# Making the two one-hots of the gates on VectorE eight tokens at a time, with the gate multiplied in on ScalarE

## The chip, the cores and the metric

The kernel runs on one NeuronCore of one Trainium2 chip. The metric is the device time of one execution in microseconds. The core has five engines that matter here, each with an instruction queue of its own that is worked off in order: TensorE (PE, matrix products, with PEld for its weight loads), VectorE (DVE), ScalarE (ACT), GpSimd (POOL), and SyncE (SP), which only issues transfers. GpSimd issues transfers as well: the indirect fetches of this kernel.

## The reference

One layer of a hybrid encoder: attention and RWKV heads, an output projection, and then a PEER block, which is the part that matters here. For each of 1024 tokens, 8 heads each choose 16 of 16384 experts, so that a token has 128 experts with a number and a softmax weight each:

```
e_idx = i1 * 128 + i2                        # per token, 8 heads x 16
gate = jax.nn.softmax(top_s, axis=-1)
u = jnp.take(expert_u, ic, axis=0)
act = jax.nn.gelu(jnp.einsum('cd,ced->ce', xc, u), approximate=False)
vv = jnp.take(expert_v, ic, axis=0)
y = jnp.einsum('ce,ced->cd', gc * act, vv)
```

All inputs and outputs are float32.

## The kernel before, in words

The kernel computes the PEER block in two ways side by side. For the first three blocks of 128 tokens (`NGB = 3`) it fetches the rows of the chosen experts with indirect transfers, one expert of 128 tokens at a time. `fetch` (L1357) issues such a transfer on GpSimd, and VectorE then makes a dot product of 1024 columns per row of U (L1390) and adds a multiple of each row of V to `gacc` (L1398). For the other five blocks (640 tokens) it computes the activations of all 16384 experts as dense products (`act_half`, L1453) and multiplies them by a dense matrix of gates, which is zero where a token did not choose an expert.

That matrix of gates, `Gd` in DRAM, is made in a stage of its own, L1672 to L1762, called the gates stage below. `g_steps(b)` handles one block of 128 tokens. `prep` splits an expert's number into its upper and lower seven bits, transposes both and the gates on TensorE and copies them to the tile `tT`. Then 16 groups of eight tokens follow:

- `hot(t8)` makes, for each of the eight tokens, two one-hot matrices of 128 slots by 128 columns. `o2` has a one where the column is the lower half of the number. `o1` has the gate where the column is the upper half. `io128` holds 0 to 127 in each partition.
- `mm(t8)` multiplies `o1` by `o2` token by token on TensorE (L1733). The product is the token's 128 by 128 matrix of gates. ScalarE copies four tokens' results at a time from PSUM to the tile `st` (L1736), and after four groups SP stores `st` to `Gd` in eight pieces (L1745).

In the kernel before, `o2` is one VectorE instruction for eight tokens (L1706). `o1` is made token by token as the string `MIX = "DDDDPPAA"` tells: four tokens on VectorE and two on GpSimd with one compare-and-multiply each (L1712), and two on ScalarE with an absolute difference (L1718) and a rectified line (L1722), for which `prep` also writes the negated numbers and gates to `tT` (L1699, L1700). Both one-hots have `NHOT = 2` buffers, so `hot(k + 2)` can start only when `mm(k)` has read its tiles. The order of issue is `hot(k + 1)` ahead of `mm(k)`.

`merge` (L1761) lays three lists over the stage: the 80 groups, the dense products of the last 20 early tiles (`A(e2, NEARLY)`, 24 products of 128x128 by 320 columns three times over for each half tile, in L315 to L317), and 60 steps of fetched experts. Each such step has one fetch of U and one of V. A fetch is issued two steps ahead in the program (`LAG`). It also gets an ordering edge to the last instruction that was put into `pace[0]`: in the gates stage that is the last GpSimd one-hot (L1715), in the stage ahead of it the last `oe` product (L1628), in the stage behind it the last `gate` product (L1786). The edge orders instructions on GpSimd's queue and is no wait between engines.

After the gates stage the dense products with V begin (`one`, L1815), which load `Gd` back (`g_load`), multiply it in on GpSimd (`gate`) and run until the end of the kernel, with the rest of the fetches beside them.

Of the kernel before, what the change touches and what calls it, by code (L numbers as in the profile page):

```python
# [8 lines left out]
F32 = mybir.dt.float32  # L9
# [4 lines left out]
AF = mybir.ActivationFunctionType  # L14
ALU = mybir.AluOpType
# [5 lines left out]
D = 1024  # L21
# [46 lines left out]
TC = 32  # L68
NSTB = 2
STQ = 0  # L70
MIX = "DDDDPPAA"
HD = 64


# [5 lines left out]
def body(tc, nc, I, out, dbg=None):  # L80
# [3 lines left out]
    with root:  # L84
# [63 lines left out]
        def slot(name, shape=(128, 1024), dt=F32):  # L148
            return sp[1].tile(list(shape), dt, name=name, tag="s")
# [11 lines left out]
        def acp(o_, i_):  # L161
            nc.scalar.activation(o_, i_, AF.Copy)  # L162
# [56 lines left out]
        for k in range(NK):  # L219
            for i in range(2):  # L220
                a = slot("adw")
# [10 lines left out]
        for tb in range(NB):  # L232
# [5 lines left out]
            if tb % 4 == 3:  # L238
                r_ = rstd[:, tb - 3:tb + 1]
# [30 lines left out]
        def merge(*parts):  # L270

            o = []
            for n_, (steps, a_, b_) in enumerate(parts):
                for i, f in enumerate(steps):
                    o.append((a_ + (b_ - a_) * (i + 0.5) / len(steps), n_, i, f))
            for _, _, _, f in sorted(o, key=lambda z: z[:3]):
                f()
# [1011 lines left out]
        for tb in range(NB):  # L1289
# [7 lines left out]
            if tb % 2:  # L1297
                r_ = ss2[:, tb - 1:tb + 1]
                nc.vector.tensor_scalar(r_, r_, 1.0 / D, 1e-6, op0=ALU.mult, op1=ALU.add)
                rsqrt(r_, r_, [128, 2], "r1")  # L1300
                for b in range(tb - 1, tb + 1):
                    h_ = tl[f"h{b}"]
                    for hf in range(2):
                        cs_ = slice(hf * 512, hf * 512 + 512)
                        nc.vector.scalar_tensor_tensor(h_[:, cs_], h2[b][:, cs_], ss2[:, b:b + 1], sc2[hf],
                                                       op0=ALU.mult, op1=ALU.mult)
# [39 lines left out]
        io128 = pid.tile([128, 128], F32, name="io128")  # L1346
# [73 lines left out]
        pace = [None]  # L1420
# [54 lines left out]
        with ES() as qs:  # L1475
# [4 lines left out]
            def qbank(name):  # L1480
                return pq.tile([128, 512], F32, name=name, tag="b")
# [19 lines left out]
            pt = qbank("pt")  # L1501
# [164 lines left out]
            A = lambda a, b: sum(tl_[a:b], [])  # L1666
# [7 lines left out]
        with ES() as gs:  # L1674
            g1 = gs.enter_context(tc.tile_pool(name="g1", bufs=2, reuse_waits=TW))
            pg_ = gs.enter_context(tc.tile_pool(name="pgs", bufs=4, space=PSUM, reuse_waits=TW))

            stores = []
            if NXG:
                more.append((g1, NXG))  # L1680

            def g_steps(b):
                tb = NGB + b
                s = {}

                def prep():
                    ij = g1.tile([128, 2, 128], I32, name="ij", bufs=1)
                    nc.vector.tensor_scalar(ij[:, 0], eid[tb], 7, None, op0=ALU.logical_shift_right)
                    nc.vector.tensor_scalar(ij[:, 1], eid[tb], 127, None, op0=ALU.bitwise_and)
                    fj = g1.tile([128, 2, 128], F32, name="fj", bufs=1)  # L1690
                    nc.vector.tensor_copy(fj, ij)
                    pt = pg_.tile([128, 512], F32, name="ptg", tag="b")
                    nc.tensor.transpose(pt[:, 0:128], fj[:, 0], ident)
                    nc.tensor.transpose(pt[:, 128:256], fj[:, 1], ident)
                    nc.tensor.transpose(pt[:, 256:384], wgt[tb], ident)

                    s["t"] = tT = g1.tile([128, 5, 128], F32, name="tT")
                    acp(tT[:, 0:3].rearrange("p a b -> p (a b)"), pt[:, 0:384])
                    nc.scalar.activation(tT[:, 3], pt[:, 256:384], AF.Copy, scale=-1.0)  # L1699
                    nc.scalar.activation(tT[:, 4], pt[:, 0:128], AF.Copy, scale=-1.0)  # L1700

                def hot(t8):
                    tT = s["t"]
                    t0 = t8 * 8
                    s[t8] = o1, o2 = [g1.tile([128, 8, 128], F32, name=n_, bufs=NHOT) for n_ in ("o1", "o2")]
                    nc.vector.tensor_tensor(o2, io128[:, None, :].to_broadcast([128, 8, 128]),  # L1706
                                            tT[:, 1, t0:t0 + 8, None].to_broadcast([128, 8, 128]), ALU.is_equal)
                    for q in range(8):
                        t = t0 + q
                        if MIX[q] != "A":  # L1710
                            eng = nc.vector if MIX[q] == "D" else nc.gpsimd
                            r_ = eng.tensor_scalar(o1[:, q], io128, tT[:, 0, t:t + 1], tT[:, 2, t:t + 1],  # L1712
                                                   op0=ALU.is_equal, op1=ALU.mult)
                            if MIX[q] == "P":
                                pace[0] = r_  # L1715
                        else:

                            nc.scalar.activation(o1[:, q], io128, AF.Abs, bias=tT[:, 4, t:t + 1])  # L1718
                    for q in range(8):
                        t = t0 + q  # L1720
                        if MIX[q] == "A":
                            nc.scalar.activation(o1[:, q], o1[:, q], AF.Relu, scale=tT[:, 3, t:t + 1],  # L1722
                                                 bias=tT[:, 2, t:t + 1])

                def mm(t8):
                    if t8 % (TC // 8) == 0:
                        s["st"] = g1.tile([128, 128, TC], F32, name="st", bufs=NSTB)
                    st = s["st"]
                    o1, o2 = s[t8]
                    for x_ in range(2):  # L1730
                        pg = pg_.tile([128, 512], F32, name="pgb", tag="b")
                        for q in range(4):
                            nc.tensor.matmul(pg[:, q * 128:(q + 1) * 128], o1[:, 4 * x_ + q], o2[:, 4 * x_ + q],  # L1733
                                             start=True, stop=True)
                        t0 = t8 * 8 % TC + x_ * 4
                        nc.scalar.activation(st[:, :, t0:t0 + 4], pg.rearrange("p (q j) -> p j q", q=4), AF.Copy)  # L1736
                    for f in stores[:NPOP]:
                        f()
                    del stores[:NPOP]
                    if t8 * 8 % TC == TC - 8:  # L1740
                        stores.extend(lambda i=i: store(st, i, 128 // TC * b + t8 * 8 // TC) for i in range(NST))

                def store(st, i, c):
                    w = TC // NST
                    (nc.scalar if STQ else nc.sync).dma_start(  # L1745
                        Gd[w * i:w * i + w, :, c].rearrange("j i a t -> i j (a t)"),
                        st[:, TA * w * i:TA * w * i + TA * w].rearrange("p (j a) t -> p j (a t)", a=TA))

                L = [prep]
                for t8 in range(15 + NHOT):  # L1750
                    if t8 < 16:
                        L.append(lambda t8=t8: hot(t8))
                    if t8 >= NHOT - 1:
                        L.append(lambda t8=t8: mm(t8 - NHOT + 1))
                return L

            def flush():
                for f in stores:
                    f()

            merge((sum([g_steps(b) for b in range(ND)], []) + [flush], 0, WG[0]), (A(e2, NEARLY), WG[1], 1),  # L1761
                  (G_(NG3 - LAG) + [more.clear] + G_(LAG), 0, WG[2]))  # L1762
# [153 lines left out]
```

## Time and profile before

| what | value |
| --- | --- |
| time, median of 3 runs | 3918.12 us (3916.42 to 3923.77) |
| the profiled execution's own time | 3917.25 us |
| its span, first to last instruction | 3915.5 us |
| TensorE's mean granted clock | 0.925 of full speed |
| PE, PEld, DVE, ACT, POOL busy over the span | 85%, 75%, 77%, 32%, 49% |
| gates stage, first one-hot to last copy of gates | 1919.2 to 2349.6 us, 430.4 us |
| POOL, DVE, PE, ACT busy in it | 399.9, 353.9, 337.9, 239.2 us |

The shares of the whole span hide the stages. The gates stage is an eleventh of the span and the only part that the change touches; there the order of the engines is another than over the whole: GpSimd is the busiest. A busy time in the windows view counts time in which at least one instruction of the engine ran, so that instructions that overlap are counted once. In the groups by line, "mean ns" is the length of one instruction, overlap included.

### The profile page before, as it was taken

The page shows a single profiled execution, that of the slowest core. Times are in us where ns is not written, and L with a number is a line of the kernel's source. Part 1 is how long each engine was busy: PE and PEld are TensorE (multiplying, and loading weights), DVE is VectorE, ACT ScalarE, POOL GpSimd, SP SyncE. Part 2 cuts the span into 40 slices and gives each one's busy share as a digit, 9 for nine tenths or more (in the row PEclk, how much of TensorE's full clock was granted, in tenths as well). Part 3 has the DMA queues.
Part 4 walks back from the last instruction along what each step waited for, and adds up shares of the span by engine and source line. Part 5 has one row for each costly group of instructions (what it writes and reads, how often), then busy time and mean ns, then how long its engine had stood idle before and what let it go on. Part 6 is the DMA issues. An engine that isn't in the chain of part 4 may idle for free. (4 is left out here: it accounts for less than half of the span.)

```text
span 3915.5 us, 59807 instructions
## 1 busy us (share of the span) xinstructions
PE 3337.0 (85%) x21937; PEld 2929.5 (75%) x21937; DVE 3016.5 (77%) x6210; ACT 1248.9 (32%) x2400; POOL 1929.2 (49%) x1506
## 2 busy tenths in 40 slices
PE   5968899899697978878778777898999889998898
PEld 4747877777586978878777776777777777777777
DVE  6785557667647899999988886777777877788776
ACT  3234344445213322222355552222222222222221
POOL 2132111221334365456799996555555655555541
PEclk9988999899798988998999898999999999999999
DMA  6443434443455366566688889777777877777774
GB/s 198 178 135 123 141 95 121 101 105 94 110 185 190 97 213 219 170 218 227 209 287 282 280 288 328 285 282 290 294 292 293 300 284 290 295 297 298 291 269 158
DMA packets 493454, 862.68 MB, mean 220 GB/s; under 512 B 149348, under 2 KB 290404, under 8 KB 489064
## 3 DMA queue, kind: packets, MB, share of 16 engines
q1 hardware_dynamic: 372840, 447.20, 35.3%
q0 software_dynamic: 113280, 411.63, 28.9%
q8 instruction: 173, 2.83, 0.3%
q10 hardware_dynamic: 7040, 0.03, 0.1%
q14 instruction: 121, 0.99, 0.1%
HBM read 741.91 MB, written 116.80 MB: 219 GB/s over the span
## 5 line engine op out<-in xcount | busy, mean ns | idle before, releaser
L317 PE MATMUL pact<-dTh,uTl 128*128 128x320 f32 x2048 | 650.3, 319 | 51.6 <-DVE uTl L1450 51.4
L315 PE MATMUL pact<-dTh,uTh 128*128 128x320 f32 x2048 | 652.6, 319 | 10.1 <-ACT gl L1461 6.1
L316 PE MATMUL pact<-dTl,uTh 128*128 128x320 f32 x2048 | 648.3, 317 | 0.0
L1390 DVE SCALAR_TENSOR_TENSOR gu<-gu,ghr 128x1024 f32<-128x1024 f32 x384 | 505.0, 1316 | 162.8 <-DMA gu<-in_peer_u_dram,ei 150.4
L1827 PE MATMUL py<-vh,ah 128*128 128x512 f32 x1280 | 523.7, 410 | 93.1 <-DVE yac L1836 64.3
L1398 DVE SCALAR_TENSOR_TENSOR gacc<-gv,gact,gacc 128x1024 f32<-128x1024 f32 x381 | 533.3, 1400 | 72.4 <-DMA gv<-in_peer_v_dram,ei 67.5
L1828 PE MATMUL py<-vl,ah 128*128 128x512 f32 x1280 | 527.6, 412 | 64.1 <-DVE vl L1807 63.5
L1362 POOL DMA_INDIRECT gu<-in_peer_u_dram,ei x384 | 504.0, 1313 | 123.6 <-issue 65.8
L1829 PE MATMUL py<-vh,al 128*128 128x512 f32 x1280 | 519.8, 406 | 3.7 <-DVE al L1788 3.7
L1362 POOL DMA_INDIRECT gv<-in_peer_v_dram,ei x384 | 457.4, 1191 | 131.4 <-issue 103.0
L317 PEld LDWEIGHTS pact<-dTh,uTl 128*128 128x128 f32 x2048 | 397.9, 195 | 58.3 <-DVE uTl L1450 58.2
L315 PEld LDWEIGHTS pact<-dTh,uTh 128*128 128x128 f32 x2048 | 398.9, 195 | 15.5 <-ACT gl L1461 8.0
L316 PEld LDWEIGHTS pact<-dTl,uTh 128*128 128x128 f32 x2048 | 398.6, 195 | 2.5
L1827 PEld LDWEIGHTS py<-vh,ah 128*128 128x128 f32 x1280 | 252.9, 198 | 154.9 <-issue 37.0
L1828 PEld LDWEIGHTS py<-vl,ah 128*128 128x128 f32 x1280 | 253.8, 198 | 140.0 <-DVE vl L1807 88.9
L1829 PEld LDWEIGHTS py<-vh,al 128*128 128x128 f32 x1280 | 253.5, 198 | 58.2 <-DVE al L1788 4.5
L1806 ACT ACTIVATE vh<-vr 128x512 fp32r<-128x512 f32 x256 | 156.0, 625 | 392.3 <-PE py L1829 361.9
L1733 PE MATMUL pgb<-o,o 128*128 128x128 f32 x1280 | 194.7, 300 | 80.7 <-POOL o L1712 76.8
L1712 POOL TENSOR_SCALAR o<-io,tT 128x128 f32<-128x128 f32 x160 | 244.5, 1533 | 11.7 <-ACT tT L162 9.3
L1733 PEld LDWEIGHTS pgb<-o,o 128*128 128x128 f32 x1280 | 174.3, 208 | 97.3 <-POOL o L1712 92.3
L1787 ACT ACTIVATE ah<-gl 128x640 fp32r<-128x640 f32 x128 | 91.2, 735 | 439.6 <-POOL gl L1786 302.9
L1788 DVE TENSOR_TENSOR al<-gl,ah 128x640 fp32r<-128x640 f32 x128 | 103.7, 830 | 130.3 <-ACT ah L1787 130.3
(1443 smaller groups left out, 7244.7 us busy)
## 6 DMA issues: line engine op xcount, KB each, us to landing
u<-in_peer_ut_dram SPq DMA_DIRECT2D x128, 512.0 KB
vr<-in_peer_v_dram SPq DMA_DIRECT2D x256, 256.0 KB
Gd<-st SPq DMA_DIRECT2D x160, 256.0 KB
actd<-gl SPq DMA_DIRECT2D x65, 320.0 KB
gl<-actd SPq DMA_DIRECT2D x65, 320.0 KB
awt<-in_ada_w_dram SPq DMA_DIRECT2D x32, 512.0 KB
wraw<-in_peer_w_query_dram SPq DMA_DIRECT2D x32, 512.0 KB
wraw<-in_w_in_dram SPq DMA_DIRECT2D x26, 512.0 KB
```

The costliest lines, as they stand in the source:

```text
L315: nc.tensor.matmul(ps, lh, rh, start=(i == 0), stop=False)
L316: nc.tensor.matmul(ps, lh, rl, start=False, stop=False)
L317: nc.tensor.matmul(ps, ll, rh, start=False, stop=(i == n - 1))
L1362: g_ = nc.gpsimd.indirect_dma_start(out=r_, out_offset=None, in_=src, in_offset=bass.IndirectOffsetOnAxis(ap=eid[tb][:, j:j + 1], axis=0))
L1390: nc.vector.scalar_tensor_tensor(u, u, 1.0, hr, op0=ALU.mult, op1=ALU.mult, accum_out=act[:, q:q + 1])
L1398: nc.vector.scalar_tensor_tensor(acc, v, pact[:, q:q + 1], acc, op0=ALU.mult, op1=ALU.add)
L1712: r_ = eng.tensor_scalar(o1[:, q], io128, tT[:, 0, t:t + 1], tT[:, 2, t:t + 1], op0=ALU.is_equal, op1=ALU.mult)
L1733: nc.tensor.matmul(pg[:, q * 128:(q + 1) * 128], o1[:, 4 * x_ + q], o2[:, 4 * x_ + q], start=True, stop=True)
L1806: nc.scalar.activation(vh, vts[i], AF.Copy)
L1827: nc.tensor.matmul(ys[hf][b], ah[:, ts], vh, start=(n == tiles[0]), stop=False)
L1828: nc.tensor.matmul(ys[hf][b], ah[:, ts], vl, start=False, stop=False)
L1829: nc.tensor.matmul(ys[hf][b], al[:, ts], vh, start=False, stop=(n == tiles[-1]))
```

## The change

`o1` and `o2` become two VectorE instructions of the same form, each for eight tokens: `o1` then holds a plain one-hot. ScalarE multiplies the gate in, in place, with eight instructions per group, one per token, each with the token's column of `tT` as its scale. GpSimd makes no one-hots any more, and so `pace[0]` isn't set in the stage. `prep` no longer writes the two negated copies, and `tT` has three parts instead of five. The groups, the buffers, the products, the stores and the order of the lists are as they were.

```diff
-MIX = "DDDDPPAA"
...
-                    s["t"] = tT = g1.tile([128, 5, 128], F32, name="tT")
-                    acp(tT[:, 0:3].rearrange("p a b -> p (a b)"), pt[:, 0:384])
-                    nc.scalar.activation(tT[:, 3], pt[:, 256:384], AF.Copy, scale=-1.0)
-                    nc.scalar.activation(tT[:, 4], pt[:, 0:128], AF.Copy, scale=-1.0)
+                    s["t"] = tT = g1.tile([128, 3, 128], F32, name="tT")
+                    acp(tT.rearrange("p a b -> p (a b)"), pt[:, 0:384])
...
-                    nc.vector.tensor_tensor(o2, io128[:, None, :].to_broadcast([128, 8, 128]),
-                                            tT[:, 1, t0:t0 + 8, None].to_broadcast([128, 8, 128]), ALU.is_equal)
+
+                    for i, o_ in enumerate((o1, o2)):
+                        nc.vector.tensor_tensor(o_, io128[:, None, :].to_broadcast([128, 8, 128]),
+                                                tT[:, i, t0:t0 + 8, None].to_broadcast([128, 8, 128]), ALU.is_equal)
                     for q in range(8):
-                        t = t0 + q
-                        if MIX[q] != "A":
-                            eng = nc.vector if MIX[q] == "D" else nc.gpsimd
-                            r_ = eng.tensor_scalar(o1[:, q], io128, tT[:, 0, t:t + 1], tT[:, 2, t:t + 1],
-                                                   op0=ALU.is_equal, op1=ALU.mult)
-                            if MIX[q] == "P":
-                                pace[0] = r_
-                        else:
-
-                            nc.scalar.activation(o1[:, q], io128, AF.Abs, bias=tT[:, 4, t:t + 1])
-                    for q in range(8):
-                        t = t0 + q
-                        if MIX[q] == "A":
-                            nc.scalar.activation(o1[:, q], o1[:, q], AF.Relu, scale=tT[:, 3, t:t + 1],
-                                                 bias=tT[:, 2, t:t + 1])
+                        nc.scalar.activation(o1[:, q], o1[:, q], AF.Copy, scale=tT[:, 2, t0 + q:t0 + q + 1])
```

## Rows read from the trace of the kernel before

**Rows 1.** Windows view: busy us of each engine, PE clock, DMA share, GB/s.

```profile
1800.00:1915.00 115.00, 95.54 (x576) 92.96 (x576) 115.00 (x267) 30.14 (x46) 70.18 (x43) 0.91 0.67 224
...
2100.00:2200.00 100.00, 79.42 (x514) 75.25 (x512) 83.68 (x142) 55.78 (x128) 92.86 (x65) 0.88 0.88 277
...
2350.00:2450.00 100.00, 78.96 (x394) 68.22 (x392) 67.57 (x76) 28.29 (x48) 62.72 (x45) 0.88 0.92 332
...
2600.00:3000.00 400.00, 360.01 (x1762) 307.28 (x1763) 313.88 (x416) 91.67 (x153) 228.64 (x176) 0.96 0.79 292
```

**Rows 2.** The same view of the whole gates stage: PE, PEld, DVE, ACT, POOL.

```profile
1919.20:2349.60 430.40, 337.91 (x2225) 318.56 (x2225) 353.88 (x609) 239.18 (x556) 399.94 (x278) 0.91 0.86 276
```

**Rows 3.** Groups by line, 1915 to 2352: count, busy us, mean ns, idle before.

```profile
L1712 POOL TENSOR_SCALAR o<-io,tT 128x128 f32<-128x128 f32 x160 | 244.5, 1533 | 11.7 <-ACT tT L162 9.3 <-issue 0.3
...
L1712 DVE TENSOR_SCALAR o<-io,tT 128x128 f32<-128x128 f32 x320 | 100.2, 401 | 0.0
L1706 DVE TENSOR_TENSOR o<-io,tT 128x1024 f32<-128x1024 f32 x80 | 98.5, 1231 | 40.0 <-PE pgb L1733 27.7 <-issue 7.0 <-ACT tT L162 5.4
L1736 ACT ACTIVATE st<-pgb 128x512 f32<-128x512 f32 x160 | 94.6, 594 | 153.9 <-PE pgb L1733 148.8 <-POOL o L1712 2.8 <-issue 1.4
L1362 POOL DMA_INDIRECT gv<-in_peer_v_dram,ei x59 | 81.3, 1378 | 18.0 <-issue 15.2 <-DVE o L1712 1.2 <-DVE o L1706 0.9
...
L1362 POOL DMA_INDIRECT gu<-in_peer_u_dram,ei x59 | 74.8, 1269 | 10.0 <-issue 8.5 <-DVE o L1712 1.3 <-PE pgb L1733 0.2
...
L1700 ACT ACTIVATE tT<-ptg 128x128 f32<-128x128 f32 x5 | 1.4, 289 | 0.0
```

**Rows 4.** Waits, 1915 to 2352: who waited for whom, us, times, longest.

```profile
PEld pgb L1733 <- POOL o L1712: 92.3, 76, 3.5
...
DVE o L1706 <- PE pgb L1733: 27.7, 22, 3.1
...
DVE gacc L1398 <- DMA gv<-in_peer_v_dram,ei: 14.2, 14, 2.6
DVE gu L1390 <- DMA gu<-in_peer_u_dram,ei: 13.3, 8, 2.2
```

**Rows 5.** GpSimd's timeline, 2130 to 2200: start, us, instructions, idle before.

```profile
2134.46 7.88 POOL L1712 TENSOR_SCALAR o<-io,tT 128x128 f32<-128x128 f32 x4
2142.51 2.13 POOL L1362 DMA_INDIRECT gu<-in_peer_u_dram,ei  x1 [0.17 <-issue]
2144.94 1.98 POOL L1362 DMA_INDIRECT gv<-in_peer_v_dram,ei  x1 [0.30 <-issue]
```

**Rows 6.** Windows view of the instructions on tile o: PE, PEld, DVE, ACT, POOL.

```profile
1919.20:2349.60 430.40, 194.68 (x1280) 174.34 (x1280) 191.59 (x400) 115.91 (x320) 244.54 (x160) 0.91 0.86 276
```

**Rows 7.** Timeline of all engines, 2100 to 2135: one group's one-hots.

```profile
2109.32 1.30 DVE L1706 TENSOR_TENSOR o<-io,tT 128x1024 f32<-128x1024 f32 x1
...
2113.94 0.69 ACT L1718 ACTIVATE o<-io,tT 128x128 f32<-128x128 f32 x2
...
2120.47 1.23 DVE L1706 TENSOR_TENSOR o<-io,tT 128x1024 f32<-128x1024 f32 x1 [2.25 <-PE pgb L1733]
...
2121.55 0.87 ACT L1722 ACTIVATE o<-o,tT 128x128 f32<-128x128 f32 x2
2121.62 1.16 DVE L1712 TENSOR_SCALAR o<-io,tT 128x128 f32<-128x128 f32 x4
```

**Rows 8.** Instructions of single lines in the stage: ns min/median/max.

```profile
L1718 ACT ACTIVATE o<-io,tT x160: 385/392/426, 1919.7 to 2340.8; 128x128 f32<-128x128 f32 x160
...
L1722 ACT ACTIVATE o<-o,tT x160: 477/482/507, 1920.3 to 2341.5; 128x128 f32<-128x128 f32 x160
...
L1706 DVE TENSOR_TENSOR o<-io,tT x80: 1205/1218/1522, 1920.0 to 2339.7; 128x1024 f32<-128x1024 f32 x80
```

**Rows 9.** Groups by line over the whole span: plain and scaled copies on ScalarE.

```profile
L1449 ACT ACTIVATE uTh<-u 128x1024 fp32r<-128x1024 f32 x128 | 135.0, 1056 | 207.0 <-PE pact L316 185.4 <-DMA vr<-in_peer_v_dram 5.9 <-DMA u<-in_peer_ut_dram 5.0
...
L246 ACT ACTIVATE xx<-xx,rstd 128x1024 f32<-128x1024 f32 x4 | 4.3, 1136 | 2.6 <-DVE rstd L104 2.6
```

## The prediction

> **What bounds the kernel now.** The page's shares over the whole span say little about this change, since it touches one stage only. I read in this order: the windows view in stretches of about 100 us, to see which engine leads where; then the groups and the waits of the gates stage; then GpSimd's timeline in it.
>
> The windows show three kinds of stretch [rows 1]. From 1800 to 1915 us VectorE is busy all the time (115.00 of 115). From 2100 to 2200, inside the gates stage, GpSimd leads with 92.86 of 100, VectorE has 83.68, TensorE 79.42. From 2600 on TensorE leads with 360 of 400. Between these two, from 2350 to 2450, the transfer engines are at their fullest, a share of 0.92 [rows 1]. So the kernel's bound changes hands, and in the gates stage it is GpSimd: 399.9 us busy of 430.4 [rows 2]. Of that 244.5 us are the 160 one-hots of 1533 ns each, and 156.1 us the 118 fetches of 1378 and 1269 ns [rows 3]. The fetches also have 28 us of idle time in front of them, nearly all "issue", that is no wait for anybody [rows 3]. 400 + 28 is 428: GpSimd's queue is full from end to end. Its timeline shows the same: one-hots, 0.17 us, a fetch, 0.30 us, a fetch, one-hots [rows 5]. And the others wait for it: TensorE's weight loads 92.3 us for a GpSimd one-hot in 76 waits [rows 4], then ScalarE's copies 148.8 us for TensorE's products [rows 3], and VectorE's `o2` 27.7 us for the tile that the late products still hold [rows 4]. That is the chain in this stage: GpSimd, product, copy, buffer.
>
> **The change part by part**, for the 430.4 us of the stage, 80 groups.
>
> GpSimd: 160 one-hots go, 244.5 us. It keeps 155.4 us of fetches and some 28 us of issue: 183 us [rows 2, 3]. Nothing that it does then bounds the stage. Its queue holds only fetches, and a fetch no longer stands behind one-hots: it goes out when its buffer is free. So transfers start earlier, on the same 16 engines as SP's stores of `st`, its loads of `u` and its stores of activations. The bytes are the same.
>
> VectorE: all instructions on the one-hots take 191.6 us of it now [rows 6], 2.39 us a group: the wide compare, 1.22 us (median), then four narrow ones. In the timeline the four start 0.08 us before the wide one has ended (2120.47 + 1.23 against 2121.62) [rows 7]. After: two wide compares of the form that L1706 has already, 1.22 + 1.22 - 0.08 = 2.36 us a group, 188.8 us. VectorE's sum goes from 353.9 to 351.1: no change. The four narrow compares were nearly as dear as one wide one, and that is why the move costs VectorE nothing. Bounds by the row of L1706 [rows 8]: 2 x 1.205 to 2 x 1.30 (the longer one in [rows 7]), less the 0.08, so 186 to 202 us, or 348 to 364 us in all.
>
> A rule can be weighed here. The row shows narrow compares on VectorE of 401 ns mean [rows 3] where four in a chain take 1.16 us [rows 7], and one-hots on GpSimd of 1533 ns. The Trainium skill, page "SBUF — State Buffer", section "Who interferes with whom", says that VectorE and GpSimd share one port pair and that an instruction of one can hold it against the other. By that rule the stretched lengths come from each other, and VectorE's sum would fall a little further, towards the lower end above; by the rows it stays at 351. No row here tells the port from other causes.
>
> ScalarE: now 115.9 us on one-hots [rows 6], 1.45 us a group. After: eight scaled copies of 128 columns. The trace has none of this shape. The nearest are L1718 (one operand from a column of `tT`, 392 ns) and L1722 (two such operands, in place, 482 ns) [rows 8]. That a scale from memory costs a copy 80 ns is also seen at 1024 columns, 1136 against 1056 ns [rows 9]. The new copy has one such operand, so I take L1718's price. Two of them take 0.69 us, two of L1722's kind 0.87 us [rows 7]; the second starts 0.30 and 0.39 us after the first. Eight in a row: 0.39 + 7 x 0.30 = 2.49 us, 199 us for 80 groups; by L1722's price 0.48 + 7 x 0.39 = 3.21 us, 257 us. `prep` loses ten short copies of 289 ns (L1700; L1699 is alike), 3 us [rows 3]. ScalarE's sum goes from 239.2 to 239.2 - 115.9 - 3 + 199 = 319 us, at most 377 us. It has 191 us of idle time, nearly all of it spent waiting for products that waited for GpSimd.
>
> The wait that is added: ScalarE's eight copies wait for VectorE's `o1`. Queued behind them on ScalarE are the copies of the previous group to `st`, the gelu of the dense products and the splits of `u`; TensorE waits for these (a PSUM bank, the next `u`), and SP's stores wait for `st`. VectorE's `o1` waits, as `o2` does now, for the products of two groups before; behind it stand the dot products of the fetched rows.
>
> Does the loop over the two buffers allow a shorter group? A group takes 430.4 / 80 = 5.38 us now. The loop: `o1` 1.22, eight copies 2.49, products still to run after the last copy some 0.5 (estimated from the cadence of 1280 products in 194.7 us [rows 6], 0.15 us each, with three or four left). That is 4.2 us for two groups, 2.1 us a group. There is much slack for the 24 dense products that can stand in between.
>
> Transfers: busy 0.86 of 430.4 us, 370 us [rows 2]. At 276 GB/s that is 119 MB. If a packet's price can't change, no stage shorter than 370 us is possible; at the rate that is reached from 2350 to 2450, 332 GB/s [rows 1], it is 358 us.
>
> What is late next: VectorE 351, transfers 358 to 370, TensorE 338, ScalarE 319, GpSimd 183. Five things within 15% of each other don't overlap wholly. VectorE's idle time is 430.4 - 353.9 = 76.5 us now: 27.7 for tiles held by late products, 27.5 for fetched rows [rows 4], the rest at the stage's start, at the blocks' starts and in issue. The first goes for the most part, of the second some half (fetches go out earlier, but on fuller transfer engines), the rest of 21 stays, and some 10 us come in for ScalarE's turn. That leaves 45 us, and 351 + 45 = 396: the stage is 34 us shorter. From the other side, 370 us of transfers in 396 us is a share of 0.93, slightly more than the 0.92 of the fullest stretch, so I give back 2 us: 32 us.
>
> Behind the stage TensorE leads at 0.90 busy [rows 1] and does the same work, with the same number of fetches left. So the gain goes through to the end. The profiled execution took 3917.25 us, 1.75 more than its span and 0.9 below the median of the runs. 3917.25 - 32 = 3885.
>
> **The rivals.**
> 1. *ScalarE becomes the stage's chain, at the low price.* For: all eight tokens of `o1` now pass through it, in order with copies that wait for TensorE. Of its 191 us of idle time only the 92.3 us that TensorE's loads waited for GpSimd would go, and 99 stay: 319 + 99 = 418 us, 12 us won, 3905. Against: much of those 99 us is waiting that a faster product shortens as well.
> 2. *The same at the high price: slower.* If an in-place scaled copy keeps L1722's spacing, ScalarE needs 377 us, and with the same 99 us of waits the stage is 476 us, 46 us longer: 3963. It decides from 430.4 - 377 = 53 us of waits on. Against: L1722 has two operands from memory, the new copy one.
> 3. *The transfer engines fill and take what GpSimd gave.* Fetches in bulk delay `u` and `st`, and VectorE waits for rows in its stead: the stage stays within 8 us of 430, about 3915. For: 0.88 busy already. Against: 332 GB/s right behind the stage.
> 4. *Everything overlaps better*: the stage falls to the transfer bounds of 358 to 370 us, 60 to 72 us won: 3845 to 3857. TensorE's clock speaks for it: 0.91 in the stage with gaps, 0.96 behind it where TensorE is 90% busy [rows 1, 2]; 338 us of TensorE would become 320. Against: no stage reaches such a coverage with this many engines near the bound.
>
> That the change does not do what it says is hardly possible: GpSimd's one-hots are gone by construction.
>
> **How the numbers follow.** The main case, 385 to 410 us of stage, 3872 to 3897: 0.53. Rival 1, 3897 to 3910: 0.16. Rival 3, 3910 to 3925: 0.11. Rival 2 and lesser forms of it, above 3925: 0.13. Rival 4, below 3872: 0.07. What a measurement of this kernel can tell from no change is 0.2%, about 8 us. Faster: 0.53 + 0.16 + 0.07 = 0.76; same 0.11; slower 0.13. The range for 8 in 10 leaves out the slower rival and the far part of rival 4: 3858 to 3925. The likeliest case alone is 3872 to 3897.
>
> **What would show it.** GpSimd in the stage at some 180 us with nobody waiting for its one-hots. VectorE with 160 wide compares of 1.22 us and 88% busy. Scaled copies of about 0.39 us, 0.30 us apart; 0.39 apart means rival 2. TensorE's waits in L1733 fall well below 92 us and name ScalarE's `o`. Transfers above 0.9 with VectorE's waits for `gu` and `gv` below 30 us; well above 60 us means rival 3. The stretch from the last copy of gates to the end keeps its 1566 us; if that moves by more than 10 us, the step "the gain goes through" is wrong. If VectorE waits long for L1733 in `o1`, the buffers' loop was not slack.

## The result, and the profile after

The changed kernel took 3868.51 us in the median of four runs (3864.69 to 3871.46) against 3917.27 us of the kernel before in the same comparison: a ratio of 0.9871, 95% interval 0.9856 to 0.9887. The forecast was 3885 with a range of 3858 to 3925. The direction and the stage were right; the gain was half as large again as the 32 us forecast, and the time lies in the case "below 3872", to which the forecast gave 0.07, not in the likeliest one (3872 to 3897). The profiled executions took 3917.25 and 3867.33 us, 49.9 us apart.

The changed kernel has one line fewer ahead of the stage and 15 fewer behind it: L1705 makes both one-hots, L1708 is the scaled copy, L1718 the product, L1721 the copy to `st`, L1730 its store, L1361 the fetch, L1438 and L1448 the load of `u` and its split on ScalarE, L1389 and L1397 the work on the fetched rows. Shown next is the windows view of the changed kernel: one stretch inside the gates stage, the stage from its first one-hot to its last copy of gates, and all that follows. The columns are PE, PEld, DVE, ACT, POOL, then TensorE's clock, the transfer engines' share and GB/s.

```profile
2100.00:2200.00 100.00, 88.44 (x633) 86.95 (x631) 96.89 (x105) 86.53 (x244) 59.02 (x34) 0.95 1.03 340
...
1919.30:2298.80 379.50, 314.81 (x2219) 306.62 (x2218) 339.15 (x365) 306.35 (x865) 196.12 (x111) 0.92 0.93 311
2298.80:3865.20 1566.40, 1387.60 (x6826) 1191.79 (x6824) 1208.38 (x1564) 356.59 (x599) 863.97 (x640) 0.96 0.77 283
```

Against [rows 1, 2]: the stage went from 430.4 to 379.5 us, 50.9 less, which is the whole gain. What follows the stage takes 1566.4 us; before it was 3915.5 - 2349.6 = 1565.9. VectorE leads now, with 96.89 of 100 in a good stretch and 339 of 379.5 over the stage. GpSimd fell from 400 to 196 us.

The groups by line, from 1905 to 2310, that answer to [rows 3]:

```profile
L1708 ACT ACTIVATE o<-o,tT 128x128 f32<-128x128 f32 x640 | 194.2, 395 | 15.6 <-DVE o L1705 15.4
L1705 DVE TENSOR_TENSOR o<-io,tT 128x1024 f32<-128x1024 f32 x160 | 187.0, 1217 | 34.2 <-ACT tT L161 24.8 <-PE pgb L1718 9.1
...
L1361 POOL DMA_INDIRECT gv<-in_peer_v_dram,ei x60 | 109.8, 1830 | 47.9 <-DVE gacc L1397 31.7 <-DVE o L1705 10.7 <-issue 4.0
...
L1361 POOL DMA_INDIRECT gu<-in_peer_u_dram,ei x60 | 97.6, 1627 | 113.5 <-DVE gu L1389 103.7 <-DVE gacc L1397 4.6 <-issue 3.7
L1721 ACT ACTIVATE st<-pgb 128x512 f32<-128x512 f32 x160 | 89.3, 593 | 17.7 <-PE pgb L1718 15.4 <-issue 0.6
...
L1448 ACT ACTIVATE uTh<-u 128x1024 fp32r<-128x1024 f32 x21 | 22.2, 1059 | 34.4 <-DMA u<-in_peer_ut_dram 32.3 <-PE pact L315 1.9
```

The scaled copies took 395 ns and 194 us in all, the wide compares 1217 ns and 187 us: both at the price that the forecast gave them. ScalarE's copies to `st` wait 15.4 us for TensorE where they waited 148.8 [rows 3]. A fetch no longer stands behind anything: it waits until VectorE has freed its buffer (103.7 and 31.7 us). One line is new in kind: the split of `u` on ScalarE waits 32.3 us for its load. Before, the profile shows no wait of it for a load in this stage. What that does is seen in the timeline of the changed kernel around its longest case:

```profile
2016.19 1.61 SPq L1730 DMA_DIRECT2D Gd<-st  x2
...
2017.91 3.43 SPq L1438 DMA_DIRECT2D u<-in_peer_ut_dram  x1
...
2029.21 1.06 ACT L1448 ACTIVATE uTh<-u 128x1024 fp32r<-128x1024 f32 x1 [10.51 <-DMA u<-in_peer_ut_dram]
2030.17 4.76 ACT L1708 ACTIVATE o<-o,tT 128x128 f32<-128x128 f32 x16
2030.61 6.73 PE L1718 MATMUL pgb<-o,o 128*128 128x128 f32 x32 [10.64 <-ACT o L1708]
2034.43 2.36 DVE L1705 TENSOR_TENSOR o<-io,tT 128x1024 f32<-128x1024 f32 x2 [9.12 <-PE pgb L1718]
...
2038.21 1.75 POOL L1361 DMA_INDIRECT gu<-in_peer_u_dram,ei  x1 [11.94 <-DVE gu L1389]
```

SP issues the load of `u` at 2017.91, behind the stores of `st`. ScalarE has reached the split and stands for 10.5 us, with two groups' scaled copies (x16) queued behind it. TensorE waits for these, VectorE for TensorE, and GpSimd for VectorE. Of VectorE's 40 us of idle time in the stage, 34 are the two entries in its row above (24.8 and 9.1), and some 28 of them follow such waits: the 9.12 us above, 5.46 us for `tT` behind the wait of 6.56 us at 1987.0, and the longest, 13.40 us for `tT`, behind the wait of 9.54 us at 2073.6.

### The profile page after: what moved, and what is told of

It reads as the page before. It is cut to its first block, busy times and chain, and to the rows that moved or that the text cites. A ratio compares the mean times of both kernels' runs of the same rounds, so it can differ in the third digit from the quotient of the medians.

```text
span 3865.2 us, 59635 instructions
## 1 busy us (share of the span) xinstructions
PE 3298.5 (85%) x21937; PEld 2906.7 (75%) x21937; DVE 3004.1 (78%) x5970; ACT 1317.4 (34%) x2710; POOL 1754.6 (45%) x1346
## 5 line engine op out<-in xcount | busy, mean ns | idle before, releaser
L1361 POOL DMA_INDIRECT gu<-in_peer_u_dram,ei x384 | 532.2, 1386 | 221.9 <-DVE gu L1389 135.2
L1389 DVE SCALAR_TENSOR_TENSOR gu<-gu,ghr 128x1024 f32<-128x1024 f32 x384 | 510.1, 1329 | 154.9 <-DMA gu<-in_peer_u_dram,ei 148.3
L1361 POOL DMA_INDIRECT gv<-in_peer_v_dram,ei x384 | 499.2, 1300 | 158.5 <-issue 89.0
L1397 DVE SCALAR_TENSOR_TENSOR gacc<-gv,gact,gacc 128x1024 f32<-128x1024 f32 x381 | 526.5, 1382 | 54.1 <-DMA gv<-in_peer_v_dram,ei 51.1
L1705 DVE TENSOR_TENSOR o<-io,tT 128x1024 f32<-128x1024 f32 x160 | 187.0, 1217 | 34.2 <-ACT tT L161 24.8
L1718 PE MATMUL pgb<-o,o 128*128 128x128 f32 x1280 | 178.4, 295 | 39.0 <-ACT o L1708 29.6
L1448 ACT ACTIVATE uTh<-u 128x1024 fp32r<-128x1024 f32 x128 | 135.1, 1056 | 215.6 <-PE pact L315 174.3
```

The costliest lines, as they stand in the source:

```text
L1361: g_ = nc.gpsimd.indirect_dma_start(out=r_, out_offset=None, in_=src, in_offset=bass.IndirectOffsetOnAxis(ap=eid[tb][:, j:j + 1], axis=0))
L1389: nc.vector.scalar_tensor_tensor(u, u, 1.0, hr, op0=ALU.mult, op1=ALU.mult, accum_out=act[:, q:q + 1])
L1397: nc.vector.scalar_tensor_tensor(acc, v, pact[:, q:q + 1], acc, op0=ALU.mult, op1=ALU.add)
L1705: nc.vector.tensor_tensor(o_, io128[:, None, :].to_broadcast([128, 8, 128]), tT[:, i, t0:t0 + 8, None].to_broadcast([128, 8, 128]), ALU.is ...
```

## The experiments

All stage lengths below are taken as in the table before: first instruction on the one-hots to the end of the last copy of gates. The bounds of the windows are up to 1 us off the exact ends in some runs: by the exact ends the stage is 379.4 us in the changed kernel, 342.2 in e2, 368.2 in e1 and 376.9 in e6. No reading rests on so little.

| kernel | time, us | ratio to before, 95% interval | stage, us | DVE, ACT, POOL busy in it |
| --- | --- | --- | --- | --- |
| before | 3917 to 3922 | | 430.4 | 354, 239, 400 |
| the change | 3868.5 | 0.9856 to 0.9887 | 379.5 | 339, 306, 196 |
| e2 GpSimd's tokens to ScalarE | 3824.1 | 0.9739 to 0.9771 | 343.2 | 332, 330, 167 |
| e3 change, GpSimd kept busy | 3981.1 | 1.0138 to 1.0172 | 481.8 | 350, 311, 453 |
| e10 before, no edge | 3914.6 | 0.9977 to 1.0010 | 434.3 | 350, 238, 398 |
| e9 three, one, four | 3917.9 | 0.9981 to 1.0008 | 428.7 | 329, 332, 300 |
| e11 the same, no edge | 3871.4 | 0.9848 to 0.9897 | 379.7 | 328, 331, 322 |
| e4 change, fetches held to groups | 3893.4 | 0.9911 to 0.9958 | 408.3 | 344, 311, 335 |
| e1 change without scaled copies | 3861.9 | 0.9837 to 0.9869 | 369.0 | 339, 130, 190 |
| e6 change, dearer copies | 3867.9 | 0.9849 to 0.9881 | 377.4 | 345, 357, 200 |
| e5 change, `u` loaded earlier | 3838.4 | 0.9771 to 0.9828 | 350.7 | 339, 306, 200 |
| e8 change, `u` loaded by ScalarE | 3843.7 | 0.9782 to 0.9824 | 350.8 | 339, 304, 197 |
| e12 e5 and e6 together | 3865.4 | 0.9828 to 0.9881 | 372.5 | 344, 357, 193 |

**Is it GpSimd's full queue?** The first theory (A): the stage was as long as GpSimd's queue, so whoever takes its work over wins, whatever the form. Run e2 leaves all as before but for the two tokens, and with them goes the ordering edge of the fetches, since only GpSimd's tokens set `pace[0]`; e10 below takes the edge alone.

```diff
-MIX = "DDDDPPAA"
+MIX = "DDDDAAAA"
```

> The kernel before with one edit: GpSimd's two tokens of eight go to ScalarE as well (two instructions each). VectorE's work is as before, ScalarE gets 116 us more (239 to 355), GpSimd keeps its fetches alone. Theory A (GpSimd's full queue was the price of the stage, and any engine with room will do): stage 380 to 400 us, time 3868 to 3888. Rival D (the two wide compares are what won): within 10 us of the time before, 3917.

Theory A held, and by more than it gave: 3824 us, the fastest kernel of the study, 44 us below the changed one. The windows row of e2's stage, then a part of its groups:

```profile
1911.30:2254.50 343.20, 301.82 (x2187) 290.09 (x2185) 331.60 (x607) 329.52 (x876) 167.41 (x112) 0.96 1.01 344
```

```profile
L1722 ACT ACTIVATE o<-o,tT 128x128 f32<-128x128 f32 x320 | 134.3, 523 | 0.0
L1718 ACT ACTIVATE o<-io,tT 128x128 f32<-128x128 f32 x320 | 104.6, 430 | 0.1
...
L1712 DVE TENSOR_SCALAR o<-io,tT 128x128 f32<-128x128 f32 x320 | 89.7, 352 | 0.0
```

VectorE and ScalarE are both busy for 96 to 97% of the stage. VectorE's 320 narrow compares, the same instructions as before, take 352 ns in the mean in place of 401 [rows 3]: without GpSimd's compares beside them, all its work on the one-hots takes 179.9 us in place of 191.6 [rows 6].

Run e3 is the opposite: the changed kernel with GpSimd's load back, for nobody.

```diff
+                    jd = g1.tile([128, 2, 128], F32, name="jd")
+                    for q in range(2):
+                        pace[0] = nc.gpsimd.tensor_scalar(jd[:, q], io128, tT[:, 0, t0 + q:t0 + q + 1],
+                                                          tT[:, 2, t0 + q:t0 + q + 1], op0=ALU.is_equal, op1=ALU.mult)
```

> The changed kernel with GpSimd's two compare-and-multiply instructions per group put back, into a scratch tile that nobody reads, and with the ordering edge of the fetches to them as before. Theory A (a full queue on GpSimd is enough, through the fetches that stand behind): GpSimd 245 + 155 to 196 + 28 us of issue, so a stage of 425 to 450 us, VectorE waiting for fetched rows, time 3910 to 3940. Rival E (it was TensorE's direct wait for GpSimd's one-hots that cost the time): nobody waits for these, the stage stays within 12 us of 380, time 3860 to 3880. By the way: if VectorE's wide compares get longer than 1.22 us, GpSimd's work holds them up.

It became slower than the kernel before, 482 us of stage. Nobody waits for these compares, so TensorE's direct wait (rival E) isn't needed to explain the length of the stage before. The waits of e3, from 1926.5 to 2408.3, show by which way a full queue bites, and the groups show why 425 to 450 was too short:

```profile
ACT o L1708 <- DVE o L1705: 115.7, 28, 8.0
PEld pgb L1722 <- ACT o L1708: 109.6, 32, 9.0
PE pgb L1722 <- DVE o L1705: 98.6, 25, 8.8
DVE gu L1389 <- DMA gu<-in_peer_u_dram,ei: 97.7, 21, 7.9
...
DVE gacc L1397 <- DMA gv<-in_peer_v_dram,ei: 32.4, 18, 3.1
```

```profile
L1705 DVE TENSOR_TENSOR o<-io,tT 128x1024 f32<-128x1024 f32 x160 | 189.6, 1234 | 1.4 <-PE pgb L1722 1.4
...
L1711 POOL TENSOR_SCALAR jd<-io,tT 128x128 f32<-128x128 f32 x156 | 305.9, 1966 | 11.3 <-ACT tT L161 9.3
```

VectorE waits 130 us for fetched rows, and the others wait for VectorE. GpSimd's compares took 1966 ns in place of 1533 [rows 3] beside VectorE's wide ones: 306 us in place of the 245 that I had put in. The wide compares took 1234 ns in place of 1217: GpSimd's work hardly holds them up. Behind the stage e3 took 1577 us, 11 more than the changed kernel; that part isn't explained.

Run e10 takes only the ordering edge away from the kernel before.

```diff
-                            if MIX[q] == "P":
-                                pace[0] = r_
```

> The kernel before without the ordering edge of the fetches to GpSimd's one-hots; the one-hots themselves stay. Theory A (GpSimd's queue is full, 400 us of work and 28 us of issue in 430): the order within the queue is of no account, stage 422 to 435 us, time 3908 to 3925. Rival J (what costs is that fetches stand behind one-hots that wait): fetches go ahead, VectorE's 27 us of waits for rows go, stage 395 to 415, time 3882 to 3904.

Theory A again. VectorE's waits for fetched rows nearly went (1.0 and 3.5 us), but its wait for tiles that TensorE still held grew from 27.7 to 62.1 us, and the time stayed. In this full queue the order of the work decided only who waits. The edge, which the change removes by the way, was worth nothing there.

```profile
PEld pgb L1731 <- POOL o L1712: 86.7, 62, 4.0
PE pgb L1731 <- POOL o L1712: 74.1, 58, 3.8
DVE o L1706 <- PE pgb L1731: 62.1, 37, 4.0
```

**Is it the full queue alone?** Run e9 deals three tokens to VectorE, one to GpSimd and four to ScalarE, and e11 does the same without the edge.

```diff
-MIX = "DDDDPPAA"
+MIX = "DDDPAAAA"
```

> The kernel before with the eight tokens dealt three to VectorE, one to GpSimd, four to ScalarE. Against the run with four, none and four (3824 us, stage 343 us, VectorE 332, ScalarE 330 of it) VectorE has 22 us less and GpSimd 80 one-hots of 1.5 to 2.0 us more: 167 + 122 to 157 + 28 us of issue, 317 to 352. Theory A in its stronger form (any one-hot in front of the fetches delays rows and products, and GpSimd at over nine tenths of the stage sets it again): stage 350 to 375, time 3830 to 3855. Rival I (only the largest sum counts, here ScalarE's 330): stage 335 to 345, time 3815 to 3826.

> Three tokens to VectorE, one to GpSimd, four to ScalarE, without the ordering edge of the fetches. With the edge this deal came to a stage of 429 us though GpSimd was busy for 300 us only, so a full queue doesn't explain that one. Rival J (fetches behind one-hots that wait for their turn in the buffers' loop, VectorE behind the rows): without the edge fetches run ahead, the waits for rows (74 us with the edge) fall below 20 us, stage 345 to 375, time 3825 to 3858. Rival K (any one-hot on GpSimd in the loop of the two buffers is the cost, since it is late and TensorE waits for it): stage 400 and more, time above 3885.

Here theory A in its simple form fell. With one token on GpSimd the time is that of the kernel before, though GpSimd is busy for only 300 of 429 us (the profiled execution, 3899.5 us, was the fastest of this kernel's runs). Without the edge the same deal has a stage of 379.7. The rows of GpSimd's compares with the edge and, below, without it:

```profile
L1712 POOL TENSOR_SCALAR o<-io,tT 128x128 f32<-128x128 f32 x80 | 138.7, 1735 | 100.6 <-issue 56.2 <-PE pgb L1733 15.9 <-ACT tT L162 9.3
```

```profile
L1712 POOL TENSOR_SCALAR o<-io,tT 128x128 f32<-128x128 f32 x80 | 149.7, 1871 | 23.4 <-PE pgb L1731 14.4 <-ACT tT L162 1.9 <-issue 1.8
```

With the edge the compares stand idle for 100 us, the fetches stand behind them in order, and VectorE waits 74 us for rows (60.1 and 13.5). Without it that falls to 4.8 us, as rival J had it. But TensorE's weight loads still wait 52.8 us for the one compare, as rival K had it, and the stage lies between what the two gave. VectorE's wait with the edge, then the two waits without it:

```profile
DVE gu L1390 <- DMA gu<-in_peer_u_dram,ei: 60.1, 28, 6.0
```

```profile
PEld pgb L1731 <- POOL o L1712: 52.8, 30, 4.5
...
DVE gu L1390 <- DMA gu<-in_peer_u_dram,ei: 4.8, 4, 1.5
```

So a queue that isn't full can cost as much as a full one, when transfers stand in it behind instructions that wait.

Run e4 asks the same of the changed kernel: a GpSimd instruction of 8 columns per group, and the fetches behind it.

```diff
+                    jd = g1.tile([128, 8], F32, name="jd")
+                    pace[0] = nc.gpsimd.tensor_scalar(jd, o2[:, 0, 0:8], tT[:, 0, t0:t0 + 1],
+                                                      tT[:, 2, t0:t0 + 1], op0=ALU.is_equal, op1=ALU.mult)
```

> The changed kernel with one tiny GpSimd instruction of 8 columns per group, which reads o2 and so waits for VectorE, and the ordering edge of the fetches to it as before: fetches go out with their groups and don't run ahead until the buffers are full. Rival H (fetches that run ahead fill the transfer engines and make u late): the wait for u falls below 10 us, stage 350 to 365 us, time 3840 to 3855. Theory F: the loads of u stay behind the stores on SP, 8 to 13 us ahead of their use, time 3860 to 3885.

The stage grew to 408 us. The wait for `u` went down only to 19.9 us, so rival H explains at most a part of it, and holding the fetches back cost VectorE 44.7 us of waits for rows (14.5 and 30.2), where the changed kernel has 1.1. It grew more than theory F gave, and the tiny instruction itself is not cheap (below): GpSimd is busy for 335 us. Holding the fetches behind the groups costs part of the gain; how much of that is the order and how much the length of the tiny instruction, this run doesn't tell apart. Its waits, from 1921.7 to 2330.0:

```profile
POOL jd L1710 <- DVE o L1705: 40.6, 10, 12.6
...
DVE gacc L1397 <- DMA gv<-in_peer_v_dram,ei: 30.2, 19, 4.3
...
ACT uTh L1448 <- DMA u<-in_peer_ut_dram: 19.9, 3, 7.6
...
DVE gu L1389 <- DMA gu<-in_peer_u_dram,ei: 14.5, 15, 3.0
```

**What is late next?** Run e1 leaves out the scaled copies (and so the gates), e6 makes them dearer.

```diff
-                    for q in range(8):
-                        nc.scalar.activation(o1[:, q], o1[:, q], AF.Copy, scale=tT[:, 2, t0 + q:t0 + q + 1])
```

> The changed kernel without the eight scaled copies on ScalarE: the gates are not multiplied in (left out), o1 stays a plain one-hot. Theory A (VectorE leads the stage at 339 of 379.5 us, and most of its 40 us of idle time comes from ScalarE standing in front of the copies until a load of u lands, 32 us in 8 waits): the products no longer hang on ScalarE's queue, ScalarE falls from 306 to about 112 us, and VectorE's idle time falls to 12 to 20 us: stage 352 to 360 us, time 3840 to 3850. Rival B (the transfer engines, 0.93 busy, are the bound): no change, within 8 us of 3868. Rival C (ScalarE's own 194 us are the chain): the stage falls as under A, so this run alone does not part A from C; the run with dearer copies does.

```diff
-                        nc.scalar.activation(o1[:, q], o1[:, q], AF.Copy, scale=tT[:, 2, t0 + q:t0 + q + 1])
+                        nc.scalar.activation(o1[:, q], o1[:, q], AF.Identity, scale=tT[:, 2, t0 + q:t0 + q + 1],
+                                             bias=io128[:, 0:1])
```

> The changed kernel with each scaled copy given a second operand from memory (a bias column of zeros, same result): 0.48 us and 0.39 us apart in place of 0.39 and 0.30, so 58 us more on ScalarE, 306 to 364 of a stage of 379.5. Theory A (VectorE leads, ScalarE has 73 us to spare, of which 32 are waits for u in front of the copies): the stage grows by 10 to 30 us, time 3878 to 3898. Rival C (ScalarE's copies are the chain): it grows by the full 58 us or more, time above 3920. Rival B (transfers are the bound): within 8 us of 3868.

Both missed what theory A gave. Without 194 us of copies the stage is only 10 to 11 us shorter, and with 63 us more of them it is no longer at all. That looked like rival B, full transfer engines. But the waits spoke against it: in e1 ScalarE's wait for `u` was still there, 43.7 us, and in e6 it was all but gone, with ScalarE busy for 357 of 377 us. The row of e1:

```profile
ACT uTh L1448 <- DMA u<-in_peer_ut_dram: 43.7, 12, 7.7
```

The distance between a load of `u` on SP and the split that reads it (the n-th load belongs to the n-th split) is 8.7 to 12.6 us from 1961 to 2236 us of the changed kernel; in e6 it is mostly 24 us and more. The distance alone doesn't make the wait: in the kernel before it was 8.4 to 16 us from 1967 to 2332 us, and ScalarE's waits in front of the split are put down to TensorE there. With other lengths the instructions come to stand in another order on the queues. In e2 it is 20 to 28 us in most cases, as in this pair from its two timelines, of SP and of ScalarE:

```profile
2008.39 0.37 SPq L1439 DMA_DIRECT2D u<-in_peer_ut_dram  x1
```

```profile
2031.99 1.05 ACT L1449 ACTIVATE uTh<-u 128x1024 fp32r<-128x1024 f32 x1
```

That led to theory F: a loop sets the pace of the changed kernel's stage. ScalarE fills `st`, SP issues eight stores of it, the load of `u` goes out behind these, and ScalarE stands at the split until it lands, with the next copies behind it. Two runs break the loop in different places. In e5 the load is earlier in the program, in e8 it goes out from another queue.

```diff
                 if m in after:
                     L[0] = lambda: (u_load(after[m]), u_split(m))
+                if n in early[EARLY[1]:] and after.get(m) in after:
+                    L[2] = lambda: u_load(after[after[m]])
```

> The changed kernel, with each load of u in the gates stage issued half a tile (two groups) earlier in the program, as soon as the split that frees its buffer has been issued. In the changed kernel a load of u goes out on SP behind eight stores of st, 8.7 to 12.6 us ahead of the split on ScalarE that reads it, and ScalarE, with all scaled copies behind that split, waits 32 us for it; taking away the copies changed the stage by 10 us only, and with dearer copies the loads stood 24 to 50 us ahead and the wait was gone. Theory F (the loop ScalarE's copies to st, SP's stores, load of u, split on ScalarE sets the stage's pace): lead of 15 us and more, ScalarE's wait for u under 6 us, stage 348 to 360 us, time 3836 to 3850. Rival G (the transfer engines are full and deliver u late whenever it is issued): the wait stays, time within 8 us of 3868.

```diff
-            nc.sync.dma_start(u, Ut[n])
+            (nc.scalar if n in early[EARLY[1] + 1:NEARLY] else nc.sync).dma_start(u, Ut[n])
```

> The changed kernel, with the loads of u in the gates stage issued from ScalarE's queue in place of SP's, so that they no longer stand behind the stores of st; where in the program they are issued is unchanged. Theory F: lead above 15 us, no wait for u, stage 348 to 362 us, time 3836 to 3852. Rival G (transfers full): the wait stays, within 8 us of 3868.

Both gave theory F's time: 3838 and 3844 us, with stages of 350.7 and 350.8. The windows rows of the stage in e5 and in e8, then e5's row of the wait for `u`:

```profile
1923.10:2273.80 350.70, 307.80 (x2221) 297.58 (x2220) 339.33 (x367) 305.74 (x865) 200.28 (x111) 0.97 1.00 336
```

```profile
1922.80:2273.60 350.80, 305.75 (x2220) 295.56 (x2220) 338.81 (x365) 304.48 (x864) 197.19 (x110) 0.97 0.99 335
```

```profile
ACT uTh L1448 <- DMA u<-in_peer_ut_dram: 2.2, 2, 1.1
```

The engines' work is that of the changed kernel to within a us for VectorE and ScalarE; the wait fell from 32.3 to 2.2 us, the stage by 28.8, and VectorE is at 97%. The same bytes went through in less time, so rival G, and with it rival B, fell. One number of both expectations was wrong, the lead of 15 us and more: in e5 the loads stand mostly 7 to 16 us ahead of their use, hardly earlier than before, and in e8 6 to 32, more than half of them less than 15. In e5 two of eight stores now stand behind the load instead of ahead of it. How much of the gain comes from the earlier issue and how much from fewer stores in front isn't told apart. TensorE's clock went with it: its mean over the stage, of its two levels 1.2 and 2.4 GHz, was 0.92 of full speed in the changed kernel and 0.97 in e5 and e8, where TensorE stood idle less; TensorE's busy time fell by 7 and 9 us. The runs don't part this from the shorter waits.

Run e12 checks the reading of e6, by its edit and that of e5 together.

> The changed kernel with the loads of u half a tile earlier and with the dearer copies (a second operand from memory) together. The run with dearer copies alone kept the time, with ScalarE busy for 357 of 377 us and no wait for u; read as a cancellation, 58 us more of work against 32 us less of waits. If so, ScalarE's 357 to 364 us are the bound there and early loads bring nothing more: stage 370 to 384 us, time 3860 to 3875. If instead ScalarE's copies were not near the chain in that run, early loads bring what they brought alone (30 us): stage 345 to 358, time 3834 to 3848.

The stage is 372.5 us, 4.9 less than in e6 and within the bounds of the cancellation: ScalarE's 357 us are the bound there, and loading earlier brings little.

```profile
1928.10:2300.60 372.50, 325.27 (x2178) 304.79 (x2177) 343.94 (x370) 356.88 (x864) 193.46 (x110) 0.94 0.94 315
```

The copies do count, then, once they are dear; in the changed kernel their wait hid that.

## Why the prediction was right, point by point

- *GpSimd's full queue is the bound of the stage.* Right: e2 and e10 from one side, e3 from the other. But the sum 400 + 28 of 430 was a sign and not yet a proof: e9 took as long with 300 us of GpSimd's work. That the chain runs over TensorE's wait for the one-hots was only one of its ways; e3 shows the other, over the fetched rows.
- *VectorE pays nothing.* Right. The wide compares took 187.0 us (forecast 188.8, bounds 186 to 202). Its sum fell to 339, not 351: the work on fetched rows and splits in the stage fell by some 8 us, since fewer of them fell into the shorter stretch (58 against 59 of L1397, 18 against 20 splits), and the rest is in how instructions overlap.
- *The port.* That each stretches the other is only half borne out. GpSimd's compares are stretched: of the 160 in the kernel before, the 24 beside which VectorE stood idle for over nine tenths of their time took 780 ns in the median, and the mean of all is 1533, or 1966 beside the wide compares of e3. VectorE's are hardly so: the narrow ones took 401 ns in the mean beside GpSimd's and 352 in e2, but 342 and 343 in the median, and the wide ones of e3 1234 in place of 1217. The Trainium skill, page "SBUF — State Buffer", section "Who interferes with whom", has an instruction with two inputs in SBUF on VectorE contend with a GpSimd instruction that reads SBUF, and the wide compare of e3 is of that kind; the trace agrees for GpSimd's side. That it is the port and no other cause, no run shows. So GpSimd's 244.5 us, which filled its queue, came in good part from VectorE (160 times 780 ns would be 125 us, an estimate).
- *ScalarE's price.* Right: 390 ns in the median, eight in 2.44 us (2.49 forecast), 306 us in all (319). The row with one operand from memory was the right neighbour; being in place cost nothing. Rival 2 fell. Rival 1 had the right place, ScalarE's order, but not the size: ScalarE was the bound only with the dearer copies (e12).
- *GpSimd keeps 155 us.* Mis-sized: a fetch took 1627 and 1830 ns in place of 1269 and 1378, 196 us in the stage. Where VectorE stood idle, fetches took 948 ns in the median (e2, over the whole run), so they too are longer beside its work. It stood off the chain.
- *Transfers can't go below 358 to 370 us.* Wrong. The engines' busy time for nearly the same bytes was 370 us before, 353 (0.93 of 379.5) after, and 347 (1.01 of 343.2) in e2. Here the share of busy time was no fixed amount of work. The 2 us given back for it were wrong, and rivals 3 and 4 leaned on it. The time fell into the case of rival 4 (3868.5, below 3872) without its reason: the stage didn't fall to 370, and TensorE's mean clock in it was 0.92 after 0.91.
- *VectorE's idle time falls to 45 us.* It was 40, but of other parts. Waits for fetched rows went from 27.5 to 1.1, where I had left half; the buffers' loop was slack, as forecast (the 9.1 us for a held tile are one wait, behind a load of `u`). The list of "five things within 15%" holds four, from 319 to 370. The term that is missing in the sum is the load of `u` behind SP's stores. The forecast named the shared transfers, and rival 3 named a late `u`, but as a matter of full engines that would end the gain. It was a matter of the order in SP's queue, cost some 29 us (e5, e8), and the gain came nevertheless.
- *The gain goes through to the end.* Right: 1565.9 and 1566.4 us behind the stage.

So the mechanism was right, and the size was short by 18 us, by amounts that all fell on one side: about 12 of it VectorE's sum, 5 its idle time and 2 the transfers. Without the wait for `u` (e5) the forecast would have been short by 47. That the forecast came so near is thus luck in part: it left out a wait of some 29 us and put other terms too high by more.

## What to carry to other kernels

Where an engine's queue also issues transfers, look for instructions in it that wait for a loop: what stands behind them can be the price, and not only its busy time (e9 and e11 differ by one ordering edge, 49 us of stage and 46.5 us of time). When a bound is removed, look through the other queues for a load that stands behind stores which wait for the engine that needs the load. And a share of busy transfer engines was no floor here: compare bytes per time with the fullest stretch, and expect that even this can be beaten, as here.

## What the runs showed of the hardware that was not expected

- GpSimd's instruction of 8 columns in e4 took 383 ns at the least and 2344 ns in the median, longer than the 1370 ns median of the 128-column compares of the kernel before. Its length came from what ran beside it, not from its columns: the 12 of them beside which VectorE stood idle for over nine tenths of their time took 392 ns in the median.
- The busy share of the transfer engines in the profile exceeded 1 in stretches (1.03 from 2100 to 2200 of the changed kernel), and they moved 344 GB/s over the stage of e2, above the 332 of the fullest stretch before [rows 1].
- A load of 512 KB that SP issued behind eight stores of 256 KB had landed about 11 us later (issued at 2017.91, read from 2029.21).
